# Small matmuls of block inverses alternate between parts of the TensorE array, with another seed of the instruction order

## The chip, the cores and the metric

The kernel runs on one core of a Trainium2 chip. The metric is the device time of one execution in microseconds (us). TensorE is called PE here, VectorE DVE, ScalarE ACT, GpSimd POOL, and SP is the queue that issues the DMAs.

## What is computed

A trunk of two layers over x of 2048 frames by 1024 channels: layer 0 is a gated linear recurrence (RG-LRU), layer 1 a gated DeltaNet with 8 heads of width 128, worked in chunks of 64 frames in the reference. Cut to what matters here, for each head:

```python
a_mat = jnp.where(strict, jnp.einsum('bhncd,bhnmd->bhncm', k_beta, k) * decay_mask, 0.0)
t_mat = lax.linalg.triangular_solve(a_mat + eye, jnp.broadcast_to(eye, a_mat.shape),
                                    left_side=True, lower=True)
w = jnp.einsum('bhncm,bhnmd->bhncd', t_mat, k_beta * jnp.exp(g)[..., None])
u = jnp.einsum('bhncm,bhnmd->bhncd', t_mat, v_beta)
...
def step(state, inp):
    v_new = u_c - jnp.einsum('bhcd,bhde->bhce', w_c, state)
    o_c = jnp.einsum('bhcd,bhde->bhce', q_c, state) + jnp.einsum('bhcm,bhme->bhce', attn_c, v_new)
    state = state * e_c[..., None, None] + jnp.einsum('bhcd,bhce->bhde', k_c, v_new)
```

The change is in how the kernel inverts the unit triangular matrices (`t_mat`), for which it uses blocks of 128 frames.

## The kernel before

Frames are taken in two halves (`u` = 0, 1) of 1024, each half in two tiles (`i`) of 512, each tile in four blocks (`b`) of 128. The big products (`products`, L703: input projections of both layers, tiles `mm`, and output projections, tiles `mmo`) split each operand in a high and a low part and issue three 128x512 matmuls per slice of 128. They fill most of PE's queue, and everything else is put between them: the gates of layer 0 (`pg`, L835), the products of keys and queries (`pkk`, `pqk`, L1172, L1260), the recurrence over blocks (`pp`, `py`, `pS`, L1415 to L1445), and the block inverses.

The inverses of one head and one half (`u`, `h`; there are 16 such pairs) run in two threads. `inverses_thread` solves the 32x32 diagonal blocks on DVE (L1295, L1298). `levels_thread` then joins blocks: 32 to 64, and 64 to 128, for all 8 blocks of 128 (2 tiles x 4 blocks) together. It has four rounds on PE, each written to one PSUM bank (tag `c`, two buffers) and emptied by ACT and DVE before the next:

- `px` (L1337): 16 matmuls of 32x32, 8 with operands in rows 0 to 31 (`a` = 0, output in partitions 32 to 63) and 8 in rows 64 to 95 (`a` = 64, output in partitions 96 to 127). Ahead of it DVE transposes the diagonal blocks in six steps (L1330); the last two of them make the operand of `a` = 64. ACT (L1340) empties the first part, DVE (L1342) the second.
- `pr` (L1349, L1352): 24 matmuls of 32x32. `a` = 0 reads rows 32 to 63 and writes partitions 0 to 31, and L1352 reads the same rows and writes partitions 32 to 63; `a` = 64 reads rows 96 to 127 and writes partitions 64 to 95. `a` = 0 and L1352 need ACT's copy, `a` = 64 needs DVE's.
- `px2` (L1366, named `px` in the profile): 8 matmuls of 64x64, all rows 0 to 63 to partitions 64 to 127. ACT (L1368) empties tile 0, DVE (L1370) tile 1.
- `pr2` (L1376, named `pr` in the profile): 8 matmuls of 64x64, all rows 64 to 127 to partitions 0 to 63. The 4 of tile 0 need ACT's copy, the 4 of tile 1 need DVE's. DVE (L1379) and ACT (L1382) empty it.

Each fp32 matmul of the code stands as two matmul records and two weight loads in the profile, so a round of 16 shows 32.

The order of instructions on each engine is fixed when the program is built. Each piece of work is a generator, and `yield "pe", 1.02` says that the next piece needs PE for 1.02 us by the planner's table. `Weave.run` always takes the thread that can start first by its own clock, and appends its instructions to their engines' queues. `SEED` starts a random sequence that scatters the planner's durations of all engines but PE by 1% (`SPREAD`), so another seed gives another order of the whole program. On the chip each engine works through its queue in that order and waits where a semaphore says so.

Of the kernel before, what the change touches and what calls it, by code (L numbers as in the profile page):

```python
# [13 lines left out]
ALU = mybir.AluOpType  # L14
# [8 lines left out]
NTC = T // TC  # L23
TB = TC // P
# [13 lines left out]

LAG = {"pe": 0.2, "act": 0.128, "dve": 0.113, "pool": 0.034}
WEIGHTS = 0.12  # L40
SEED, SPREAD = 58, 0.01
TABLE = 1.28
TRANSFER = {"sp": (1.56, 0.61, 0.05), "st": (0.74, 0.38, 0.5)}
SHARED = {"dve2": "pool2", "pool2": "dve2"}
# [126 lines left out]
def trunk_kernel(ctx, tc, x, head, small, ada_w, ada_b, final_g, w1, gate_w, ow1, w2, wab, ow2, out):  # L171
    nc = tc.nc
    act, dve, pool, pe, sp = nc.scalar, nc.vector, nc.gpsimd, nc.tensor, nc.sync
# [87 lines left out]
    def tile_(shape, tag, name, dtype=F32):  # L261
        p, n = tags[tag]
        return pools[p].tile(shape, dtype, tag=tag, name=name, bufs=n)
# [4 lines left out]
    def ev(*key):  # L268
        return events.setdefault(key, Event())

    def put(tag, token):
        w.put(slots[tag], token)
# [553 lines left out]
    def gates_thread(u, n, i):  # L826
        xf, ftok = yield ev("xf", u, n, i)
        gw = yield ev("gw", u, n)
        if (u, n, i) == (NU - 1, KT - 1, NTC - 1):
            w.set(ev("lasthalves"))  # L830
        for g in range(2):
            ctok = yield slots["c"]
            yield "pe", 0.86
            pg = ps.tile([P, TC], F32, tag="c", name="pg")
            pe.matmul(pg, lhsT=gw[:, g, :], rhs=xf, start=True, stop=True)  # L835
            w.spawn(gate_thread(u, n, i, g, pg, ctok), 3)
        w.set(ev("gated", u, n, i))
        tr, rtok = yield ev("gate1", u, n, i, 0)
        ti, itok = yield ev("gate1", u, n, i, 1)
        htok = yield slots["th"]  # L840
        yield "act", 0.723, LAG["act"], "exp"
        th = tile_([P, TC], "th", "th")
        act.activation(th, tr, AF.Tanh, bias=sp2[:, n:n + 1], scale=sp2[:, n:n + 1])
        yield "act", 0.724, LAG["act"], "exp"
        act.activation(tr, tr, AF.Exp, bias=sp4n[:, n:n + 1], scale=sp4n[:, n:n + 1])
        yield "dve2", 0.599
        dve.scalar_tensor_tensor(th, tr, 1.0, th, ALU.add, ALU.mult)
        yield "dve2", 0.599
        dve.scalar_tensor_tensor(tr, th, 2.0, th, ALU.subtract, ALU.mult)
        yield "pool2", 0.696  # L850
        pool.tensor_scalar(th, th, -1.0, 1.0, ALU.mult, ALU.add)
        yield "dve2", 0.599
        dve.scalar_tensor_tensor(ti, ti, 1.0, xf, ALU.add, ALU.mult)
        put("xf1", ftok)
        yield "act", 0.54, LAG["act"], "sqrt"
        act.activation(tr, tr, AF.Sqrt, scale=-0.25)
        if u + i > 0:
            yield ev("hcar", n, u * NTC + i - 1)
        yield "dve2", 0.603
        dve.tensor_tensor(ti, ti, tr, ALU.mult)  # L860
        put("tg", rtok)
        yield "dve2", 1.19
        init = 0.0 if u + i == 0 else hcar[:, n:n + 1]
        dve.tensor_tensor_scan(out=ti, data0=th, data1=ti, initial=init, op0=ALU.mult, op1=ALU.add)
        put("th", htok)
        yield "pool", 0.546
        pool.tensor_copy(out=hcar[:, n:n + 1], in_=ti[:, TC - 1:TC])
        w.set(ev("hcar", n, u * NTC + i))
        tz, ztok = yield ev("tz", u, n, i)
        yield "dve2", 0.601  # L870
        dve.tensor_tensor(tz, tz, ti, ALU.mult)
        put("tg", itok)
        yield "st", 1.1
        t0 = u * T + i * TC
        sp.dma_start(out=y_d[n * P:(n + 1) * P, t0:t0 + TC], in_=tz)
        put("tz", ztok)
        w.set(ev("y", u, n, i))

    def gate_thread(u, n, i, g, pg, ctok):
        tok = yield slots["tg"]  # L880
        yield "act", 0.593, LAG["act"], "exp"
        tg = tile_([P, TC], "tg", "tg")
        act.activation(tg, pg, AF.Tanh, bias=gb_s[:, g, n:n + 1], scale=0.5)
        put("c", ctok)
        w.set(ev("gate1", u, n, i, g), (tg, tok))
# [424 lines left out]
    def levels_thread(u, h):  # L1310

        tt_d = yield ev("tt", u, h)
        acs = []
        for i in range(NTC):
            acs.append((yield ev("key", u, h, i))[2])
            for b in range(4):
                yield "sp", 0.016, i == NTC - 1 and b == 3
                q0 = b * NB + i * TB
                sp.dma_start(out=acs[i][32 * b:32 * b + 32, :, 32 * b:32 * b + 32],
                             in_=tt_d[q0:q0 + TB].rearrange("c j i -> j c i"))  # L1320
        chunks = [(i, b, acs[i][:, b, :]) for i in range(NTC) for b in range(TB)]
        ftok = yield slots["tf"]
        yield "pool", 0.391
        tf = tile_([P, NTC, TB, 64], "tf", "tf")
        pool.memset(tf[0:32, :, :, 32:64], 0.0)
        for b in range(3):
            for i in range(NTC):
                yield "dve", 0.199
                o = 32 * (b % 2)
                dve.transpose(out=tf[32 * b:32 * b + 32, i, :, o:o + 32],  # L1330
                              in_=acs[i][32 * b:32 * b + 32, :, 32 * b:32 * b + 32])
        ctok = yield slots["c"]
        yield "pe", 1.02
        px = ps.tile([P, NTC, TB, 32], F32, tag="c", name="px")
        for a in (0, 64):
            for i, b, ac in chunks:
                pe.matmul(px[a + 32:a + 64, i, b, :], lhsT=ac[a:a + 32, a + 32:a + 64],  # L1337
                          rhs=tf[a:a + 32, i, b, 0:32], start=True, stop=True)
        yield "act", 0.282
        act.activation(tf[32:64, :, :, 0:32], px[32:64], AF.Copy, scale=-1.0)  # L1340
        yield "dve", 0.349
        dve.tensor_scalar(tf[96:128, :, :, 0:32], px[96:128], -1.0, None, ALU.mult)  # L1342
        put("c", ctok)
        ctok = yield slots["c"]
        yield "pe", 1.2
        pr = ps.tile([P, 2, NTC, TB, 32], F32, tag="c", name="pr")
        for a in (0, 64):
            for i, b, ac in chunks:
                pe.matmul(pr[a:a + 32, 0, i, b, :], lhsT=tf[a + 32:a + 64, i, b, 0:32],  # L1349
                          rhs=ac[a + 32:a + 64, a + 32:a + 64], start=True, stop=True)  # L1350
                if a == 0:
                    pe.matmul(pr[32:64, 1, i, b, :], lhsT=ac[32:64, 32:64], rhs=tf[32:64, i, b, 0:32],  # L1352
                              start=True, stop=True)
        yield "act", 0.27
        act.copy(tf[32:64, :, :, 0:32], pr[32:64, 1])
        yield "act", 0.163
        act.copy(acs[0][64:96, :, 96:128], pr[64:96, 0, 0])
        for i, a in ((0, 0), (1, 0), (1, 64)):
            yield "dve", 0.197
            dve.tensor_copy(out=acs[i][a:a + 32, :, a + 32:a + 64], in_=pr[a:a + 32, 0, i])  # L1360
        put("c", ctok)
        ctok = yield slots["c"]
        yield "pe", 0.928
        px = ps.tile([P, NTC, TB, 64], F32, tag="c", name="px2")
        for i, b, ac in chunks:
            pe.matmul(px[64:128, i, b, :], lhsT=ac[0:64, 64:128], rhs=tf[0:64, i, b, :], start=True, stop=True)  # L1366
        yield "act", 0.286
        act.activation(tf[64:128, 0], px[64:128, 0], AF.Copy, scale=-1.0)  # L1368
        yield "dve", 0.347
        dve.tensor_scalar(tf[64:128, 1], px[64:128, 1], -1.0, None, ALU.mult)  # L1370
        put("c", ctok)
        ctok = yield slots["c"]
        yield "pe", 0.928
        pr = ps.tile([P, NTC, TB, 64], F32, tag="c", name="pr2")
        for i, b, ac in chunks:
            pe.matmul(pr[0:64, i, b, :], lhsT=tf[64:128, i, b, :], rhs=ac[64:128, 64:128], start=True, stop=True)  # L1376
        put("tf", ftok)
        yield "dve", 0.335
        dve.tensor_copy(out=acs[0][0:64, :, 64:128], in_=pr[0:64, 0])  # L1379
        w.set(ev("inv", u, h, 0))  # L1380
        yield "act", 0.271
        act.copy(acs[1][0:64, :, 64:128], pr[0:64, 1])  # L1382
        w.set(ev("inv", u, h, 1))
        put("c", ctok)

# [403 lines left out]
```

## Time and profile before

| what | value |
|---|---|
| median of 3 runs | 1878.76 us (1876.84 to 1879.47) |
| the profiled execution's own time | 1877.61 us |
| its span, first to last instruction | 1875.9 us |
| PE busy | 1831.7 us, 98% |
| weight loads busy | 1472.3 us, 78% |
| DVE, ACT, POOL busy | 1347.0, 1163.4, 359.6 us |
| mean granted TensorE clock | 0.995 |

A row of the timeline gives start (us), length (us), engine, line, operation, output<-inputs, shape, and a count; in brackets the engine's idle time before it and what ended it. Records of PE overlap: the next one starts before the modelled end of the last, so the distance between starts, not the length of a record, says what PE's queue paid. Rows of the same line that follow one another are merged.

### The profile page before, as it was taken

To read this page: it belongs to the slowest core of one execution; us is meant where nothing else is said; L and a number is where in the kernel's file an instruction comes from. 1 tells how busy PE (TensorE), PEld (TensorE's weight loads), DVE (VectorE), ACT (ScalarE), POOL (GpSimd) and SP (SyncE) were. 2 spreads that over 40 slices of the span, in tenths; PEclk is the share of its full clock that TensorE was granted. 3 is DMA by queue.
4 is the path that set the end of the run, shared out by engine and by line. 5 is a ranking of instruction groups with operands and counts; after the bars stand their busy time and mean duration, and the time that the engine had idled before them with its cause. 6 is when DMAs were issued, how large, how long until landed. Compare 5 with 4: busy or idle time off the path is not lost.

```text
span 1875.9 us, 30928 instructions
## 1 busy us (share of the span) xinstructions
PE 1831.7 (98%) x10222; PEld 1472.3 (78%) x10222; DVE 1347.0 (72%) x3121; ACT 1163.4 (62%) x2703; POOL 359.6 (19%) x896
## 2 busy tenths in 40 slices
PE   6999999999999999999999999999999999999998
PEld 4777777777888877887887877788888888887887
DVE  7889897776455648777788877667676677776653
ACT  4655777666211467787777766786778787754221
POOL 1111110011000013132422221131222222311010
PEclk9999999999999999999999999999999999999999
DMA  8467756554588545467677656356654655686841
GB/s 352 140 196 209 231 178 211 171 166 133 194 221 222 186 125 147 130 179 186 154 168 178 146 147 206 106 136 153 156 137 123 158 142 147 153 235 193 252 145 68
DMA packets 510425, 322.75 MB, mean 172 GB/s; under 512 B 369844, under 2 KB 437940, under 8 KB 510264
## 3 DMA queue, kind: packets, MB, share of 16 engines
q1 hardware_dynamic: 510264, 320.77, 60.6%
q8 instruction: 81, 1.33, 0.3%
q14 instruction: 80, 0.66, 0.1%
HBM read 219.93 MB, written 100.73 MB: 171 GB/s over the span
## 4 chain that ended last, share of the span: by engine, by line
PE 75%; DVE 7%; DMA 6%; ACT 6%; issue 2%; SPq 2%; POOL 2%; DVEq 0%; POOLq 0%; ACTq 0%
PE mm L703 40%; PE mmo L703 18%; DMA raw<-in_w 3%; PE pg L835 3%; DMA oraw<-in_ow 2%; PE py L1432 1%; PE pp L1415 1%; PE pS L1445 1%; PE pS L1444 1%; PE pqk L1260 1%; PE pp L1416 1%; PE adaps L372 1%; PE pkk L1172 1%; PE pab L1058 1%; DVE xf L755 1%
## 5 line engine op out<-in xcount | busy, mean ns | idle before, releaser
L755 DVE SCALAR_TENSOR_TENSOR xf<-xe,small_s,xf 128x512 f32<-128x512 f32 x288 | 214.3, 750 | 32.0 <-ACT xf L1013 28.8
L679 ACT CAST whi<-raw 128x1024 fp32r<-128x1024 f32 x96 | 100.2, 1043 | 55.5 <-DMA raw<-in_w 52.1
L1295 DVE TENSOR_TENSOR ttmp<-blk,tblk 128x60 f32<-128x60 f32 (+24 forms) x496 | 106.0, 214 | 19.4 <-DMA o_d<-ob 4.5
L1298 DVE TENSOR_TENSOR tblk<-tblk,ttmp 128x60 f32<-128x60 f32 (+24 forms) x496 | 106.3, 214 | 12.4
L703 PE MATMUL mm<-hh_('in2', 0)_4993,whi 128*128 128x512 f32 x256 | 105.2, 411 | 0.0
L703 PE MATMUL mm<-hh_('in2', 1)_11807,wlo 128*128 128x512 f32 x256 | 104.8, 409 | 0.0
L703 PE MATMUL mm<-hl_('in2', 1)_11604,whi 128*128 128x512 f32 x256 | 104.7, 409 | 0.0
L703 PE MATMUL mm<-hh_('in2', 1)_11603,wlo 128*128 128x512 f32 x256 | 104.7, 409 | 0.0
L703 PE MATMUL mm<-hh_('in2', 0)_4993,wlo 128*128 128x512 f32 x256 | 104.4, 408 | 0.0
L703 PE MATMUL mm<-hh_('in2', 1)_11603,whi 128*128 128x512 f32 x256 | 104.2, 407 | 0.0
L703 PE MATMUL mm<-hl_('in2', 0)_4994,whi 128*128 128x512 f32 x256 | 103.8, 406 | 0.0
L703 PE MATMUL mm<-hl_('in2', 1)_11808,whi 128*128 128x512 f32 x256 | 103.8, 405 | 0.0
L703 PE MATMUL mm<-hh_('in2', 1)_11807,whi 128*128 128x512 f32 x256 | 103.8, 405 | 0.0
L703 PE MATMUL mm<-hh_('in2', 0)_5108,wlo 128*128 128x512 f32 x256 | 103.5, 404 | 0.0
L703 PE MATMUL mm<-hl_('in2', 0)_5109,whi 128*128 128x512 f32 x256 | 103.0, 403 | 0.0
L703 PE MATMUL mm<-hh_('in2', 0)_5108,whi 128*128 128x512 f32 x256 | 103.0, 402 | 0.0
L703 PE MATMUL mmo<-ol,oh 128*128 128x512 f32 (+1 forms) x264 | 102.7, 389 | 0.0
L703 PE MATMUL mmo<-oh,ol 128*128 128x512 f32 (+1 forms) x264 | 102.7, 389 | 0.0
L703 PE MATMUL mmo<-oh,oh 128*128 128x512 f32 (+1 forms) x264 | 102.6, 389 | 0.0
L703 PE MATMUL mmo<-oh,yl 128*128 128x512 f32 x256 | 100.8, 394 | 0.0
L703 PE MATMUL mmo<-oh,yh 128*128 128x512 f32 x256 | 100.8, 394 | 0.0
L703 PE MATMUL mmo<-ol,yh 128*128 128x512 f32 x256 | 100.4, 392 | 0.0
(314 smaller groups left out, 5388.0 us busy)
## 6 DMA issues: line engine op xcount, KB each, us to landing
raw<-in_w SPq DMA_DIRECT2D x96, 512.0 KB, 4.2
araw<-in_ada_w SPq DMA_DIRECT2D x32, 512.0 KB, 4.4
xt<-x_d SPq DMA_DIRECT2D x32, 512.0 KB, 4.8
xt_d<-xb SPq DMA_DIRECT2D x192, 64.0 KB, 2.7
xk<-xt_d SPq DMA_DIRECT2D x24, 512.0 KB, 6.5
xt<-in_x SPq DMA_DIRECT2D x16, 512.0 KB, 5.6
ada<-in_ada_w SPq DMA_DIRECT2D x16, 512.0 KB, 10.2
y_d<-tz SPq DMA_DIRECT2D x32, 256.0 KB, 4.8
```

The costliest lines, as they stand in the source:

```text
L372: pe.matmul(pt, lhsT=c_bc[:, k, :], rhs=raw[:, k, :], start=(k == 0), stop=(k == KT - 1))
L679: act.copy(hi, raw)
L703: pe.matmul(pt, lhsT=lhs[a][:, k, :], rhs=rhs[b][:, k, :], start=(k == 0 and n == 0), stop=(k == KT - 1 and n == 2))
L755: dve.scalar_tensor_tensor(xf, xe[:, 1 + j:1 + j + TC], wc[:, j:j + 1], xf, ALU.mult, ALU.add)
L835: pe.matmul(pg, lhsT=gw[:, g, :], rhs=xf, start=True, stop=True)
L1058: pe.matmul(pab, lhsT=whl[:, k, :], rhs=hpr[q][:, k, :], start=(k == 0 and q == 0), stop=(k == KT - 1 and q == 1))
L1172: pe.matmul(pkk[:, b, :], lhsT=kc, rhs=kc, start=True, stop=True)
L1260: pe.matmul(pqk[:, b, :], lhsT=kt[:, b * P:(b + 1) * P], rhs=qt[:, b * P:(b + 1) * P], start=True, stop=True)
L1295: dve.tensor_tensor(tmp, blk[:, j, j + 1:32].unsqueeze(2).to_broadcast([P, r, c_]), t[:, j, 0:c_].unsqueeze(1).to_broadcast([P, r, c_]), A ...
L1298: dve.tensor_tensor(t[:, j + 1:32, 0:c_], t[:, j + 1:32, 0:c_], tmp, ALU.subtract)
L1415: pe.matmul(pp[:, 0, :], lhsT=kc, rhs=S_, start=True, stop=True)
L1416: pe.matmul(pp[:, 1, :], lhsT=qc, rhs=S_, start=True, stop=True)
```

## The change

The order of the matmuls in the four rounds is changed. `chunks` runs over blocks outside and tiles inside; in `px` and `pr` the two row parts (`a` = 0 and `a` = 64) follow each other for each block, where before all of `a` = 0 came first. In `px2` and `pr2` the outputs of tile 0 and tile 1 go to different partition halves of the bank, so consecutive matmuls alternate between them; DVE's L1370 then reads partitions 0 to 63 and writes 64 to 127, and ACT's L1382 reads 64 to 127 and writes 0 to 63. The planner's durations of the four rounds and of the gates are edited, and the seed is another. Number and shape of the matmuls are as before.

```diff
-SEED, SPREAD = 58, 0.01
+SEED, SPREAD = 120, 0.01
...
-            yield "pe", 0.86
+            yield "pe", 0.856
             pg = ps.tile([P, TC], F32, tag="c", name="pg")
...
-        chunks = [(i, b, acs[i][:, b, :]) for i in range(NTC) for b in range(TB)]
+        chunks = [(i, b, acs[i][:, b, :]) for b in range(TB) for i in range(NTC)]
...
-        yield "pe", 1.02
+        yield "pe", 0.7
         px = ps.tile([P, NTC, TB, 32], F32, tag="c", name="px")
-        for a in (0, 64):
-            for i, b, ac in chunks:
+        for i, b, ac in chunks:
+            for a in (0, 64):
                 pe.matmul(px[a + 32:a + 64, i, b, :], lhsT=ac[a:a + 32, a + 32:a + 64],
                           rhs=tf[a:a + 32, i, b, 0:32], start=True, stop=True)
...
-        yield "pe", 1.2
+        yield "pe", 0.92
         pr = ps.tile([P, 2, NTC, TB, 32], F32, tag="c", name="pr")
-        for a in (0, 64):
-            for i, b, ac in chunks:
+        for i, b, ac in chunks:
+            for a in (0, 64):
                 pe.matmul(pr[a:a + 32, 0, i, b, :], lhsT=tf[a + 32:a + 64, i, b, 0:32],
                           rhs=ac[a + 32:a + 64, a + 32:a + 64], start=True, stop=True)
-                if a == 0:
-                    pe.matmul(pr[32:64, 1, i, b, :], lhsT=ac[32:64, 32:64], rhs=tf[32:64, i, b, 0:32],
-                              start=True, stop=True)
+            pe.matmul(pr[32:64, 1, i, b, :], lhsT=ac[32:64, 32:64], rhs=tf[32:64, i, b, 0:32], start=True, stop=True)
...
-        yield "pe", 0.928
+        yield "pe", 0.66
         px = ps.tile([P, NTC, TB, 64], F32, tag="c", name="px2")
         for i, b, ac in chunks:
-            pe.matmul(px[64:128, i, b, :], lhsT=ac[0:64, 64:128], rhs=tf[0:64, i, b, :], start=True, stop=True)
+            pe.matmul(px[64 - 64 * i:128 - 64 * i, i, b, :], lhsT=ac[0:64, 64:128], rhs=tf[0:64, i, b, :], start=True, stop=True)
...
-        dve.tensor_scalar(tf[64:128, 1], px[64:128, 1], -1.0, None, ALU.mult)
+        dve.tensor_scalar(tf[64:128, 1], px[0:64, 1], -1.0, None, ALU.mult)
...
-        yield "pe", 0.928
+        yield "pe", 0.66
         pr = ps.tile([P, NTC, TB, 64], F32, tag="c", name="pr2")
         for i, b, ac in chunks:
-            pe.matmul(pr[0:64, i, b, :], lhsT=tf[64:128, i, b, :], rhs=ac[64:128, 64:128], start=True, stop=True)
+            pe.matmul(pr[64 * i:64 * i + 64, i, b, :], lhsT=tf[64:128, i, b, :], rhs=ac[64:128, 64:128], start=True, stop=True)
...
-        act.copy(acs[1][0:64, :, 64:128], pr[0:64, 1])
+        act.copy(acs[1][0:64, :, 64:128], pr[64:128, 1])
```

The next pieces are the programs' own order, one engine each, before any run; `[waits DVE_49]` is a wait for DVE's counter, and lines from L1352 on lie 1 to 2 lower in the changed file. PE's queue at the first `px` round, before:

```order
L703 MATMUL mm<-hl_('in2', 0)_4994,whi 128x512
L1337 MATMUL px<-tf,ac 32x32 [waits DVE_49]
L1337 MATMUL px<-tf,ac 32x32 x3
L1337 MATMUL px<-tf,ac 32x32 [waits DVE_49]
L1337 MATMUL px<-tf,ac 32x32 x3
L1337 MATMUL px<-tf,ac 32x32 [waits DVE_49]
L1337 MATMUL px<-tf,ac 32x32 x3
L1337 MATMUL px<-tf,ac 32x32 [waits DVE_49]
L1337 MATMUL px<-tf,ac 32x32 x3
L703 MATMUL mm<-hh_('in2', 0)_4993,wlo 128x512
```

The same place, now:

```order
L703 MATMUL mm<-hl_('in2', 0)_4994,whi 128x512
L1337 MATMUL px<-tf,ac 32x32 [waits DVE_49] x2
L1337 MATMUL px<-tf,ac 32x32
L1337 MATMUL px<-tf,ac 32x32 [waits DVE_49]
L1337 MATMUL px<-tf,ac 32x32 x12
L703 MATMUL mm<-hh_('in2', 0)_4993,wlo 128x512
```

The waits for the last two transposes, which stood ahead of the 9th and the 13th matmul, stand ahead of the 2nd and the 4th. PE's queue at the first `pr` round, before (the second wait for DVE is that for the operand of `a` = 64; rows between are left out):

```order
L1349 MATMUL pr<-ac,tf 32x32 [waits DMAHW6_49,Activation_49]
L1352 MATMUL pr<-tf,ac 32x32
L1349 MATMUL pr<-ac,tf 32x32
...
L1349 MATMUL pr<-ac,tf 32x32 [waits DMAHW2_49]
...
L1349 MATMUL pr<-ac,tf 32x32 [waits DMAHW0_49,DVE_49]
L1349 MATMUL pr<-ac,tf 32x32 x3
L1349 MATMUL pr<-ac,tf 32x32 [waits DMAHW4_49]
```

The same place, now:

```order
L1349 MATMUL pr<-ac,tf 32x32 [waits DMAHW6_49,Activation_49]
L1349 MATMUL pr<-ac,tf 32x32 [waits DMAHW0_49,DVE_49]
L1351 MATMUL pr<-tf,ac 32x32
L1349 MATMUL pr<-ac,tf 32x32 [waits DMAHW2_49]
L1349 MATMUL pr<-ac,tf 32x32 [waits DMAHW4_49]
L1351 MATMUL pr<-tf,ac 32x32
```

The wait for DVE moved from the 17th matmul to the 2nd. What the seed does is seen at the second `px` round on PE, where the neighbours are the recurrence of the head before. Before:

```order
L1445 MATMUL pS<-yt,at 128x128
L703 MATMUL mm<-hh_('in2', 0)_5108,whi 128x512
L703 MATMUL mm<-hl_('in2', 0)_5109,whi 128x512
L1337 MATMUL px<-tf,ac 32x32 [waits Activation_49]
L1337 MATMUL px<-tf,ac 32x32 x7
L1337 MATMUL px<-tf,ac 32x32 [waits DVE_49]
...
L1415 MATMUL pp<-state_97,kt 128x128 [waits DVE_49]
L1416 MATMUL pp<-state_97,qt 128x128
```

Now:

```order
L1413 MATMUL pp<-state_97,kt 128x128 [waits DVE_49]
L1414 MATMUL pp<-state_97,qt 128x128
...
L1430 MATMUL py<-zt,ac 128x128 [waits DMAHW1_49,DVE_49]
L1337 MATMUL px<-tf,ac 32x32 x3
L1337 MATMUL px<-tf,ac 32x32 [waits DVE_49]
L1337 MATMUL px<-tf,ac 32x32 x12
L703 MATMUL mm<-hl_('in2', 0)_4994,whi 128x512
```

The round stood ahead of a recurrence step (`pp`) and stands in the middle of one now, between `py` and `pS`; all engines' queues differ in this way from the first tile of layer 0 on.

## Prediction

> **What bounds the kernel.** I read the page's totals first, then a table by stage, then PE's waits, then the timeline of PE around single rounds.
>
> ```profile
> span 1875.9 us, 30928 instructions
> PE 1831.7 (98%) x10222; PEld 1472.3 (78%) x10222; DVE 1347.0 (72%) x3121; ACT 1163.4 (62%) x2703; POOL 359.6 (19%) x896
> ```
>
> ```profile
> core 0: us, PE busy (x) PEld busy (x) DVE busy (x) ACT busy (x) POOL busy (x), PEclk, DMA share, GB/s
> 39.00:470.00 431.00, 425.71 (x1762) 324.68 (x1761) 357.49 (x598) 284.55 (x392) 59.01 (x82) 1.00 0.59 182
> 470.00:641.00 171.00, 171.00 (x745) 139.56 (x745) 92.08 (x133) 40.82 (x51) 9.39 (x21) 1.00 0.75 219
> 641.00:1721.00 1080.00, 1063.10 (x6974) 873.02 (x6972) 788.81 (x2227) 787.11 (x2160) 267.68 (x722) 1.00 0.60 155
> 1721.00:1869.00 148.00, 147.88 (x667) 121.76 (x666) 80.37 (x93) 34.12 (x74) 15.29 (x43) 1.00 0.52 163
> ```
>
> The second table's columns are the stage, its length, each engine's busy time, PE's granted clock and the DMA share. The four stages are the input projections of layer 0, its output projection, layer 1, and the last output projection. PE stands idle 5.3 us in the first (431 less 425.71), 0, 16.9 and 0.1 us in the others, 22.3 us together. The inverses all lie in layer 1, where DVE and ACT are busy 73% of 1080 us. So PE's queue sets the time, and a microsecond less of PE work there is a microsecond of the span, as long as the other engines follow.
>
> ```profile
> PE px L1337 <- DVE tf L1330: 1.2, 2, 0.6
> PE pr L1349 <- DVE tf L1342: 1.1, 2, 0.8
> ```
>
> PE's waits in the rounds (total us, times, longest) are small now. They become important below.
>
> **What the new order of the matmuls saves.** First a `px` round that waits for nothing.
>
> ```profile
> 1675.39 0.39 PE L703 MATMUL mmo<-oh,oh 128*128 128x512 f32 x1
> 1675.71 1.09 PE L1337 MATMUL px<-tf,ac 32*32 32x32 f32 x32
> 1676.73 0.50 PE L703 MATMUL mmo<-ol,oh 128*128 128x512 f32 x1
> ```
>
> It holds PE's queue for 1676.73 - 1675.71 = 1.02 us. Then a `pr` round, start to end with rows left out:
>
> ```profile
> 1283.77 0.21 PE L1349 MATMUL pr<-ac,tf 32*32 32x32 f32 x1
> 1283.77 0.21 PE L1352 MATMUL pr<-tf,ac 32*32 32x32 f32 x1
> ...
> 1284.17 0.19 PE L1349 MATMUL pr<-ac,tf 32*32 32x32 f32 x1
> 1284.17 0.19 PE L1352 MATMUL pr<-tf,ac 32*32 32x32 f32 x1
> 1284.18 0.21 PE L1349 MATMUL pr<-ac,tf 32*32 32x32 f32 x2
> 1284.21 0.19 PE L1352 MATMUL pr<-tf,ac 32*32 32x32 f32 x1
> 1284.23 0.19 PE L1349 MATMUL pr<-ac,tf 32*32 32x32 f32 x2
> ...
> 1284.27 0.19 PE L1352 MATMUL pr<-tf,ac 32*32 32x32 f32 x1
> 1284.30 0.57 PE L1349 MATMUL pr<-ac,tf 32*32 32x32 f32 x13
> 1284.80 0.50 PE L703 MATMUL mm<-hh_('in2', 1)_11603,wlo 128*128 128x512 f32 x1
> ```
>
> This round already does in part what the change wants everywhere. L1349 with `a` = 0 and L1352 write different column parts of the array and alternate in the code: their 32 records start within 0.50 us, two every 0.032 us. The 16 records of L1349's `a` = 64, in other rows and other columns, come behind them, and three of those start before the other two parts have ended (the rows marked x2, since 13 are left for the last row). There three records start every 0.032 us and none is slowed. Afterwards the 13 that are left take 0.50 us alone. So one part of the array starts a 32x32 record every 0.032 us, parts do not hold each other up, and a part that stands behind a long run of another part starts late.
>
> `px`: two parts of 16 records, now in turn. Like the 32 above, they start within 0.50 us, and 1.02 less the 0.90 between its first and last start (1.09 less 0.19 for a record) leaves 0.12 to the next work. New 0.62, saved 0.40.
>
> `pr`: three parts of 16. All at once 0.51 + 0.12 = 0.63 against 1284.80 - 1283.77 = 1.03: saved 0.40. If only two parts ran at a time it would be 48 records at 0.016, 0.75 + 0.12, saved 0.16. I take 0.40, since the trace shows three at once.
>
> ```profile
> 1287.51 1.14 PE L1366 MATMUL px<-tf,ac 64*64 64x64 f32 x16
> 1288.59 0.50 PE L703 MATMUL mm<-hl_('in2', 1)_11604,whi 128*128 128x512 f32 x1
> ```
>
> `px2` and `pr2`: 1.08 us for 16 records, of which 1.14 less about 0.22 for one record, 0.92, lies between first and last start: 0.061 each. No row shows 64x64 records in two parts. The bounds are nothing saved, and half of the 0.92, 0.46. Nearest are the two column parts of `pr`, which share their rows just as the two halves here do and ran without loss; I take 0.46.
>
> [...]
>
> If nothing were late: 16 x (0.40 + 0.40 + 0.46 + 0.46) = 27.5 us.
>
> **What it takes away.** In the old order the first half of a round ran while the second half's operand was still made. Now the second matmul waits for it.
>
> ```profile
> 757.33 1.38 PE L1337 MATMUL px<-tf,ac 32*32 32x32 f32 x32
> 757.92 0.30 DVE L1330 STREAM_TRANSPOSE tf<-ac 32x128 f32<-32x128 f32 x1
> 758.64 0.50 PE L703 MATMUL mm<-hh_('in2', 0)_4993,wlo 128*128 128x512 f32 x1
> ...
> 1618.09 0.50 DVE L1330 STREAM_TRANSPOSE tf<-ac 32x128 f32<-32x128 f32 x2
> 1618.21 1.09 PE L1337 MATMUL px<-tf,ac 32*32 32x32 f32 x32
> 1619.24 0.50 PE L703 MATMUL mm<-hl_('in2', 1)_11604,whi 128*128 128x512 f32 x1
> ```
>
> In 8 of the 16 `px` rounds the last transpose ended after the round's first matmul had started (the first and the last of the 8 stand here): 758.22 against 757.33, late by 0.89, and 1618.59 against 1618.21, late by 0.38. The 8 latenesses sum to 6.6 us, and these rounds held PE 10.5 us in all (1.31 in the first, 1.03 in the last). With the same lateness the new round lasts the lateness plus about 0.61 (0.05 from the transpose's end to the fourth matmul, 28 records at 0.016, and the 0.12): 6.6 + 8 x 0.61 = 11.5. So late `px` rounds lose 1.0 together, and the other 8 gain 3.2: net 2.2 us instead of 6.4.
>
> ```profile
> 760.23 0.21 PE L1349 MATMUL pr<-ac,tf 32*32 32x32 f32 x1
> 760.38 0.43 DVE L1342 TENSOR_SCALAR tf<-px 32x256 f32<-32x256 f32 x1
> ...
> 1678.82 0.21 PE L1349 MATMUL pr<-ac,tf 32*32 32x32 f32 x1 [0.21 <-ACT tf L1340]
> 1679.72 0.69 PE L1349 MATMUL pr<-ac,tf 32*32 32x32 f32 x16 [0.20 <-DVE tf L1342]
> ```
>
> The same in `pr`, where `a` = 64 needs DVE's L1342: late in 4 of 16 (the first and the last stand here, 0.58 and about 0.84). Those 4 keep nearly their time (saved 0.35 together), 12 save 0.40: 5.2 us.
>
> ```profile
> 766.59 0.43 DVE L1370 TENSOR_SCALAR tf<-px 64x256 f32<-64x256 f32 x1
> 766.63 1.14 PE L1376 MATMUL pr<-ac,tf 64*64 64x64 f32 x16
> ...
> 1685.49 1.32 PE L1376 MATMUL pr<-ac,tf 64*64 64x64 f32 x16
> 1685.65 0.43 DVE L1370 TENSOR_SCALAR tf<-px 64x256 f32<-64x256 f32 x1
> ```
>
> And in `pr2`, where tile 1 needs L1370: late in 4 (first and last here, 0.39 and 0.59); 0.2 + 12 x 0.46 = 5.7 us. `px2` needs ACT's L1355 in every matmul, before and now: 16 x 0.46 = 7.4 us.
>
> Behind a wait stands PE's whole queue, which is in order, so the lateness is paid in full.
>
> **The rest.** Two evacuations (L1370, L1382) now cross partition halves. No row shows that; I take their present durations, and if each took twice its time, some 0.4 us on DVE and on ACT per pair, the idle quarter of both engines would cover it unless the round is late. The changed order adds 4 rows of table loads on ACT (121 to 125):
>
> ```profile
> L1131 ACT ACT_TABLE_LOAD x32 | 41.1, 1283 | 0.5
> ```
>
> At 1.283 us that is 5.1 us, hidden by ACT's 293 us of idle time in layer 1; without that cover it is a loss of 5.1. The seed and the planner's new durations move every instruction, DMAs of the SP queue too, but add no work. Their price lies in the 22.3 us of PE idle: a luckier order takes off at most that, an unluckier one may add as much. No row says which; I take 0, and half of it, 10 us, either way for the range.
>
> **Sum.** 2.2 + 5.2 + 7.4 + 5.7 = 20.5 us. The profiled execution took 1877.61 us for its span of 1875.9; it becomes 1857.1. The median of the three runs, 1878.76, lies 1.15 higher, so the forecast is 1858.
>
> **Rivals.**
> Nothing late (chance 0.15): the new order places the rounds where DVE is done. 27.5 us, 1851. For it: half of `px` and three quarters of `pr` are so now. Against it: an order that makes PE faster leaves DVE less time.
>
> [...]
>
> Slower (0.04): PE, faster than its neighbours, arrives at the second matmul of `px`, `pr` and `pr2` before DVE each time. There are 48 such places; from 0.43 us more lateness on average at each, the 20.5 us are gone, and at 0.6 us it is 1887. For it: `px` is late in half its rounds already. Against it: three quarters of `pr` and `pr2` are not.
>
> The new order eats most: an added idle time near 22 us gives no change (0.05), about 13 us gives 1871 (0.09).
>
> **Numbers.** The forecast itself, 1848 to 1868 with the order's 10 us, has 0.55. Faster by over 0.2% (3.8 us, about what can be told from no change here) are the forecast, nothing late, no overlap and the eaten gain: 0.55 + 0.15 + 0.12 + 0.09 = 0.91. Same 0.05, slower 0.04. The range reaches to 1871, to hold the partial cases, and down to 1847.
>
> **What would show it.** Right: undisturbed `px` rows x32 of about 0.70 us with the next work 0.62 behind their start, `pr` at 0.63, 64x64 rows x16 of about 0.68 with 0.61 to the next; records of different parts alternating; PE idle of layer 1 not far from 17 us, with more in the waits for L1330 and L1342. Wrong: 64x64 records still 0.06 us apart, or waits for DVE in the rounds of 20 us in sum, or idle elsewhere that grew with the order.

## The result: 1854 us, 1.3% faster, and the profile after

The changed kernel takes 1854.09 us (median of 4 runs, 1852.01 to 1858.81) against 1878.69 for the kernel before (4 runs): ratio 0.9874, 95% interval 0.9853 to 0.9895. The profiled execution took 1852.01 us, with a mean granted clock of 0.997. In the changed file the lines from L1351 on lie 1 to 2 lower than before: `px2` is L1364, `pr2` L1374, its operand for tile 1 comes from L1368, the recurrence is L1413 to L1443.

The page's totals after:

```profile
span 1849.5 us, 30915 instructions
PE 1805.3 (98%) x10222; PEld 1445.4 (78%) x10222; DVE 1342.6 (73%) x3121; ACT 1169.4 (63%) x2707; POOL 351.0 (19%) x896
```

PE's busy time fell by 26.4 us, the span by 26.4. The four stages of the changed kernel, in the columns of the prediction's table:

```profile
39.00:470.00 431.00, 427.78 (x1770) 325.76 (x1770) 356.89 (x600) 295.96 (x401) 50.21 (x82) 1.00 0.59 184
470.00:641.00 171.00, 171.00 (x745) 139.55 (x744) 92.24 (x132) 38.17 (x48) 8.15 (x21) 1.00 0.75 216
641.00:1697.00 1056.00, 1037.18 (x6982) 846.84 (x6982) 784.88 (x2227) 784.82 (x2158) 269.26 (x722) 1.00 0.61 159
1697.00:1843.00 146.00, 145.53 (x657) 119.80 (x655) 80.66 (x93) 33.71 (x72) 15.13 (x43) 1.00 0.49 157
```

Layer 1 lasts 1056 us where it lasted 1080; the stages ahead of it end at the same times as before. Its PE idle time is 18.8 us (1056 less 1037.18), against 16.9.

Rounds that wait for nothing, in the timeline of PE of the changed kernel:

```profile
1654.07 0.69 PE L1337 MATMUL px<-tf,ac 32*32 32x32 f32 x32
1654.69 0.50 PE L703 MATMUL mmo<-oh,oh 128*128 128x512 f32 x1
...
1662.79 0.68 PE L1364 MATMUL px<-tf,ac 64*64 64x64 f32 x16
1663.41 0.50 PE L703 MATMUL mmo<-oh,oh 128*128 128x512 f32 x1
```

`px` holds the queue for 0.62 us (1654.69 less 1654.07), where it held it for 1.02; `px2` for 0.62 where it held it for 1.08 (`pr2`, not shown, is like it: 0.61 in 11 of 16 rounds). And `pr`, with rows left out:

```profile
1107.69 0.22 PE L1349 MATMUL pr<-ac,tf 32*32 32x32 f32 x2
1107.70 0.21 PE L1351 MATMUL pr<-tf,ac 32*32 32x32 f32 x1
...
1108.20 0.19 PE L1351 MATMUL pr<-tf,ac 32*32 32x32 f32 x1
1108.32 0.50 PE L703 MATMUL mm<-hh_('in2', 0)_4993,wlo 128*128 128x512 f32 x1
```

Three records, one of each part, start every 0.032 us, from the first row to the last before L703, so the round lasts 0.63 us (1108.32 less 1107.69) instead of 1.03.

What the change took away shows too. The longest wait in a round, PE first and then DVE:

```profile
1276.21 0.32 PE L1374 MATMUL pr<-ac,tf 64*64 64x64 f32 x2
1278.07 0.68 PE L1374 MATMUL pr<-ac,tf 64*64 64x64 f32 x14 [1.54 <-DVE tf L1368]
1278.67 0.50 PE L703 MATMUL mm<-hh_('in2', 1)_11798,wlo 128*128 128x512 f32 x1
```

```profile
1276.47 0.75 DVE L755 SCALAR_TENSOR_TENSOR xf<-xe,small_s,xf 128x512 f32<-128x512 f32 x1
1277.14 0.18 DVE L1295 TENSOR_TENSOR ttmp<-blk,tblk 128x28 f32<-128x28 f32 x1
1277.36 0.21 DVE L1298 TENSOR_TENSOR tblk<-tblk,ttmp 128x28 f32<-128x28 f32 x1
1277.60 0.42 DVE L1368 TENSOR_SCALAR tf<-px 64x256 f32<-64x256 f32 x1
```

The two records of tile 0's first matmul start at 1276.21. The second matmul is tile 1's, and its operand comes from L1368, which stands on DVE behind three instructions of other threads and ends at 1278.02. The round takes 2.46 us. In the old order three more matmuls of tile 0 would have run in that time.

The sums over all 16 rounds of a kind, from a round's first record to the next other matmul (differences rounded last):

| kind | before, us | after, us | saved | forecast |
|---|---|---|---|---|
| `px` | 18.7 | 14.0 | 4.6 | 2.2 |
| `pr` | 17.3 | 12.3 | 5.1 | 5.2 |
| `px2` | 17.1 | 9.8 | 7.3 | 7.4 |
| `pr2` | 17.9 | 12.9 | 5.0 | 5.7 |
| sum | 71.0 | 49.0 | 22.0 | 20.5 |

### The profile page after: what moved, and what is told of

It is laid out like the page before. It is cut to its first block, busy times and chain, and to the rows that moved or that the text cites. A ratio compares the mean times of both kernels' runs of the same rounds, so it can differ in the third digit from the quotient of the medians.

```text
span 1849.5 us, 30915 instructions
## 1 busy us (share of the span) xinstructions
PE 1805.3 (98%) x10222; PEld 1445.4 (78%) x10222; DVE 1342.6 (73%) x3121; ACT 1169.4 (63%) x2707; POOL 351.0 (19%) x896
## 3 DMA queue, kind: packets, MB, share of 16 engines
q8 instruction: 80, 1.31, 0.3%
## 4 chain that ended last, share of the span: by engine, by line
PE 65%; DMA 10%; DVE 9%; ACT 8%; SPq 4%; issue 3%; POOL 1%; DVEq 0%; POOLq 0%; ACTq 0%
PE mm L703 34%; PE mmo L703 18%; DMA raw<-in_w 3%; PE pg L835 2%; DVE xf L755 2%; PE py L1430 1%; PE pS L1443 1%; PE pS L1442 1%; PE pp L1413 1%; PE pp L1414 1%; DMA oraw<-in_ow 1%; PE adaps L372 1%; ACT whi L679 1%; SPq L1319 1%; PE pqk L1260 1%
## 5 line engine op out<-in xcount | busy, mean ns | idle before, releaser
L679 ACT CAST whi<-raw 128x1024 fp32r<-128x1024 f32 x96 | 100.0, 1042 | 59.4 <-DMA raw<-in_w 58.8
L703 PE MATMUL mm<-hh_('in2', 1)_11798,whi 128*128 128x512 f32 x256 | 105.1, 410 | 0.0
L703 PE MATMUL mm<-hh_('in2', 1)_11579,wlo 128*128 128x512 f32 x256 | 104.4, 408 | 0.0
L703 PE MATMUL mm<-hh_('in2', 0)_4993,wlo 128*128 128x512 f32 x256 | 104.3, 407 | 0.0
L703 PE MATMUL mm<-hh_('in2', 1)_11579,whi 128*128 128x512 f32 x256 | 104.1, 407 | 0.0
L703 PE MATMUL mm<-hh_('in2', 1)_11798,wlo 128*128 128x512 f32 x256 | 104.0, 406 | 0.0
L703 PE MATMUL mm<-hl_('in2', 0)_4994,whi 128*128 128x512 f32 x256 | 104.0, 406 | 0.0
L703 PE MATMUL mm<-hh_('in2', 0)_5108,whi 128*128 128x512 f32 x256 | 103.6, 405 | 0.0
L703 PE MATMUL mm<-hl_('in2', 1)_11580,whi 128*128 128x512 f32 x256 | 103.3, 404 | 0.0
L703 PE MATMUL mm<-hh_('in2', 0)_4993,whi 128*128 128x512 f32 x256 | 103.2, 403 | 0.0
L703 PE MATMUL mm<-hh_('in2', 0)_5108,wlo 128*128 128x512 f32 x256 | 103.1, 403 | 0.0
L703 PE MATMUL mmo<-oh,oh 128*128 128x512 f32 (+1 forms) x264 | 103.0, 390 | 0.0
L703 PE MATMUL mmo<-oh,ol 128*128 128x512 f32 (+1 forms) x264 | 102.8, 389 | 0.0
L703 PE MATMUL mm<-hl_('in2', 0)_5109,whi 128*128 128x512 f32 x256 | 102.6, 401 | 0.0
L703 PE MATMUL mm<-hl_('in2', 1)_11799,whi 128*128 128x512 f32 x256 | 102.6, 401 | 0.0
L703 PE MATMUL mmo<-ol,oh 128*128 128x512 f32 (+1 forms) x264 | 102.1, 387 | 0.0
L703 PE MATMUL mmo<-oh,yh 128*128 128x512 f32 x256 | 100.8, 394 | 0.0
L703 PE MATMUL mmo<-oh,yl 128*128 128x512 f32 x256 | 100.8, 394 | 0.0
L703 PE MATMUL mmo<-ol,yh 128*128 128x512 f32 x256 | 100.3, 392 | 0.0
```

What stands on the lines that cost most here:

```text
L679: act.copy(hi, raw)
L703: pe.matmul(pt, lhsT=lhs[a][:, k, :], rhs=rhs[b][:, k, :], start=(k == 0 and n == 0), stop=(k == KT - 1 and n == 2))
```

## The experiments

The change has two parts that can be told apart: the rounds' inner order, and the order of the whole program (seed and planned durations). None of the kernels below leaves out any of the computation. Ratios are to runs of the kernel before on the same chip. To read them I split the stretch from 39 us to PE's last matmul of each profiled execution into three: PE's idle time, what PE lost while its granted clock was 0.50 (an estimate: half of the time in these stretches), and the rest, which is PE's busy time at full clock. The three add up to the length. Half of the idle time inside the stretches at 0.50 is in the clock's loss too, so the loss is too large there and the busy time at full clock too small: by 3 us with seed 200, by 7 with short plans, by 0 to 2.6 in the others.

| kernel | ratio (95% interval) | length | busy at full clock | idle | lost to the clock |
|---|---|---|---|---|---|
| before | 1 | 1829.9 | 1802.6 | 22.2 | 5.1 |
| after | 0.9874 (0.9853 to 0.9895) | 1803.5 | 1779.8 | 22.0 | 1.7 |
| alternation alone | 0.9970 (0.9956 to 0.9984) | 1820.3 | 1781.3 | 30.5 | 8.5 |
| order alone | 0.9926 (0.9908 to 0.9944) | 1817.5 | 1799.0 | 13.3 | 5.1 |
| 32-wide rounds alone | 0.9988 (0.9972 to 1.0005) | 1822.3 | 1792.9 | 22.5 | 6.8 |
| 64-wide rounds alone | 0.9969 (0.9954 to 0.9983) | 1828.3 | 1792.2 | 27.5 | 8.5 |
| old seed, new durations | 0.9971 (0.9955 to 0.9986) | 1824.9 | 1777.2 | 35.8 | 11.9 |
| new seed, old durations | 0.9963 (0.9947 to 0.9979) | 1820.3 | 1780.9 | 32.6 | 6.8 |
| seed 7 | 0.9929 (0.9902 to 0.9957) | 1817.7 | 1773.5 | 30.6 | 13.7 |
| order of seed 7, old rounds | 1.0017 (1.0004 to 1.0030) | 1830.6 | 1798.1 | 22.3 | 10.2 |
| seed 200 | 1.0047 (1.0028 to 1.0066) | 1840.2 | 1777.3 | 40.7 | 22.2 |
| order of seed 200, old rounds | 1.0142 (1.0117 to 1.0166) | 1851.9 | 1800.2 | 32.9 | 18.8 |
| short plans, seed 200 | 1.0077 (1.0061 to 1.0093) | 1845.1 | 1768.8 | 42.1 | 34.1 |

The last four columns come from one execution each, the ratios from all. The clock's loss differs between executions of one kernel by several us (the mean granted clock of 28 runs of the kernel before goes from 0.990 to 0.998), so a difference of 3.4 us in that column shows nothing by itself.

**The alternation alone.** The kernel before with the five edits of the matmuls and the two of the evacuations; seed, planned durations and so the order on every engine are those of before.

```diff
-        chunks = [(i, b, acs[i][:, b, :]) for i in range(NTC) for b in range(TB)]
+        chunks = [(i, b, acs[i][:, b, :]) for b in range(TB) for i in range(NTC)]
...
-        for a in (0, 64):
-            for i, b, ac in chunks:
+        for i, b, ac in chunks:
+            for a in (0, 64):
...
-            pe.matmul(px[64:128, i, b, :], lhsT=ac[0:64, 64:128], rhs=tf[0:64, i, b, :], start=True, stop=True)
+            pe.matmul(px[64 - 64 * i:128 - 64 * i, i, b, :], lhsT=ac[0:64, 64:128], rhs=tf[0:64, i, b, :], start=True, stop=True)
```

> The alternation of all four rounds alone: seed, planner's durations and with them every engine's order of instructions are those of before. Theory A (parts of the array run at once, PE's queue is the bound): rounds that wait for nothing take 0.62 (px), 0.63 (pr), 0.61 (px2, pr2) us, and with the latenesses of before's order the sum of my forecast holds, 20.5 us: 1858 us, range 1854 to 1865. In the late px rounds the new order is no faster than the old: the first one, at about 757 us, takes 1.4 to 1.6 us where it took 1.31. Rival B (the other seed and the planner's durations made the gain, the alternation little): 1874 to 1879 us.

Measured: 1872.05 us, ratio 0.9970. The rounds got shorter by 16.4 us (`px` 1.7, `pr` 5.0, `px2` 7.0, `pr2` 2.6), but only about 5.6 us of it arrived in the time, which lies between the ranges of both theories. PE's waits there (total us, times, longest):

```profile
PE px L1337 <- DVE tf L1330: 3.9, 7, 0.9
PE pr L1374 <- DVE tf L1368: 3.4, 5, 1.1
...
PE px L1364 <- DVE ac L1358: 2.8, 2, 2.6
...
PE py L1430 <- DVE zt L1422: 2.3, 5, 1.1
...
PE pr L1374 <- ACT tf L1366: 1.6, 1, 1.6
```

In the kernel before, in the same order, these five are 1.2, 0.2, 2.3, 0.2 and 0.3 us. The first `px` round of this kernel shows the price that the prediction worked out:

```profile
759.83 0.61 PE L1337 MATMUL px<-tf,ac 32*32 32x32 f32 x6
760.79 0.62 PE L1337 MATMUL px<-tf,ac 32*32 32x32 f32 x26 [0.35 <-DVE tf L1330]
761.35 0.50 PE L703 MATMUL mm<-hh_('in2', 0)_4993,wlo 128*128 128x512 f32 x1
```

It lasts 1.52 us (761.35 less 759.83); before it lasted 1.31. In the profiled execution PE idles 8.3 us more, and loses 3.4 us more to the clock. The second part is not borne out by all runs: their mean granted clock is 0.9939, and 0.9940 in the runs of the kernel before beside them.

**The order alone.** The changed kernel, with seed 120 and the new planned durations, but the matmuls inside the rounds as before.

```diff
-        for i, b, ac in chunks:
-            for a in (0, 64):
+        for a in (0, 64):
+            for i, b, ac in chunks:
...
-            pe.matmul(pr[64 * i:64 * i + 64, i, b, :], lhsT=tf[64:128, i, b, :], rhs=ac[64:128, 64:128], start=True, stop=True)
+            pe.matmul(pr[0:64, i, b, :], lhsT=tf[64:128, i, b, :], rhs=ac[64:128, 64:128], start=True, stop=True)
```

> The order of instructions of the changed kernel on every engine (seed 120, new planner durations), with the matmuls inside the four rounds as before (one part after the other). Theory A: rounds take 1.02, 1.03, 1.08, 1.08 us again; of the 24.6 us between the medians the rounds explain 22.0 (sums of the time they held PE, before less after), so the order alone is worth about 2.6 us: 1876, range 1871 to 1881. Rival B: 1854 to 1860 us.

Measured: 1865.12 us, ratio 0.9926, outside both ranges, with rounds that last 68.8 us in all, nearly as before (71.0). Idle time is 13.3 us. So more than half of the change's gain is there without any change in the rounds, and the alternation added to this order brings the ratio from 0.9926 to 0.9874.

**One width at a time.** In the order of before, only `px` and `pr` alternate in the one kernel, only `px2` and `pr2` in the other (the edits are those of the alternation alone, taken apart).

> Only px and pr alternate (32x32), px2 and pr2 as before; order of instructions of before. Theory A: px gains 2.2 to 4.6, pr 5.1 us: 1869 to 1872. Rival C (a round's gain is eaten by waits elsewhere, so that the parts of the change do not add up): under 4 us, 1875 to 1879.

> Only px2 and pr2 alternate (64x64, partition halves), px and pr as before; order of instructions of before. Theory A: px2 gains 7.4, pr2 5.0 to 5.7 us: 1865 to 1867, and with the experiment on the 32-wide rounds alone the gains add to that of all four. Rival C: under 6 us, 1873 to 1879.

Measured: 0.9988 for the 32-wide rounds, which can't be told from no change, and 0.9969 for the 64-wide ones. In the profiled executions PE's busy time at full clock fell by 9.7 and 10.4 us, together about the 21.3 of the alternation alone. Neither part is without effect on PE, and neither brings much of it to the end, as rival C had it.

**Seed or durations.** The changed kernel with the seed of before (58), and with the planned durations of before.

```diff
-SEED, SPREAD = 120, 0.01
+SEED, SPREAD = 58, 0.01
```

```diff
-            yield "pe", 0.856
+            yield "pe", 0.86
...
-        yield "pe", 0.7
+        yield "pe", 1.02
...
-        yield "pe", 0.92
+        yield "pe", 1.2
...
-        yield "pe", 0.66
+        yield "pe", 0.928
...
-        yield "pe", 0.66
+        yield "pe", 0.928
```

> The changed kernel (alternation, new planner durations) with the seed of before, 58. Theory D, formed on the first four runs: the alternation shortens the rounds as forecast, but where the planner still believes in the old durations PE runs ahead of its plan and the saved time comes back as waits for DVE and ACT; the planner has to be told. Then most of the gain is here with any seed: 1853 to 1863 us, PE idle in layer 1 about 15 us. Rival E (seed 120 is a lucky draw worth about 12 us): 1864 to 1872, idle about 25 us as in the alternation alone.

> The changed kernel with seed 120, but the planner's durations of before (1.02, 1.2, 0.928, 0.928, gates 0.86). Theory D: as in the alternation alone PE runs ahead of its plan: 1864 to 1874 us, late px and pr2 rounds, PE idle in layer 1 about 25 us. Rival E: 1852 to 1860.

Measured: 1873.36 and 1870.67 us, ratios 0.9971 and 0.9963. That is what the alternation gives in the order of before (0.9970). Neither the new durations nor the seed is worth anything alone: PE idles 35.8 and 32.6 us in them, and 22.0 with both. That the planner has truer durations does not make the order better. Theory D misses the first of the two by 10 us, rival E the second.

**Other seeds.** The changed kernel with seeds 7 and 200, the number being the only edit.

> The changed kernel with an arbitrary seed, 7. Theory D: 1853 to 1865 us; a draw costs a few us of PE idle. Rival E: 1864 to 1876.

> The changed kernel with another arbitrary seed, 200. Theory D: 1853 to 1865 us. Rival E: 1864 to 1876.

Measured: 1864.29 us (0.9929) and 1887.90 us (1.0047). With 120 and 58 that makes four programs that differ in one number: 1854, 1864, 1873 and 1888 us, a spread of 34 us, more than the whole change. The slowest of them is slower than the kernel before, and lies outside both ranges given for it. With the old rounds three of these orders were run (below), and they rank alike: seed 120's is the fastest, then seed 7's, and seed 200's the slowest. PE's waits with seed 200:

```profile
PE pqk L1260 <- ACT qt L1020: 6.4, 4, 3.0
PE py L1430 <- DVE zt L1422: 5.4, 8, 1.7
PE px L1337 <- DVE tf L1330: 5.0, 6, 1.7
PE pS L1442 <- ACT yt L1436: 4.1, 9, 1.0
PE pp L1413 <- DVE state L1455: 3.5, 8, 0.5
```

In the changed kernel the same five are 1.9, 1.3, 2.4, 2.2 and 0.7 us. What lies behind three of them is seen in PE's queue with seed 200:

```profile
1154.86 0.49 PE L1413 MATMUL pp<-state,kt 128*128 128x128 f32 x2 [0.44 <-DVE state L1455]
1155.19 0.39 PE L1414 MATMUL pp<-state,qt 128*128 128x128 f32 x2
1156.05 0.49 PE L1430 MATMUL py<-zt,ac 128*128 128x128 f32 x2 [0.48 <-DVE zt L1422]
1156.91 0.49 PE L1442 MATMUL pS<-yt,kd 128*128 128x128 f32 x2 [0.37 <-ACT yt L1436]
...
1160.34 0.79 PE L1442 MATMUL pS<-yt,kd 128*128 128x128 f32 x2 [0.37 <-ACT yt L1436]
```

The steps of the recurrence follow one another with no product of L703 between them, so PE waits 0.4 us for DVE or ACT at each. There are 20 such bare steps in this order, with 8.5 us of idle time; in the kernel before there is none, in the changed one there are 3, without a wait. With the old rounds the order of seed 200 has the same 20, with 8.7 us, so they come with the order and not with the alternation. From 1159 us on the records are longer (0.79 us for L1442 at 1160.34, 0.49 at 1156.91), and the clock is lower: 0.93 on average in the 5 us to 1160, 0.52 in the 10 us from there.

**Shorter plans.** Seed 200, and the planner told that the rounds take 0.3 to 0.35 us, less than they do, in the hope that the other engines get more time between them. With seed 120 the same plan gave no kernel and so no time; the expectation below means that one by "the run before".

```diff
-        yield "pe", 0.7
+        yield "pe", 0.3
...
-        yield "pe", 0.92
+        yield "pe", 0.35
...
-        yield "pe", 0.66
+        yield "pe", 0.31
...
-        yield "pe", 0.66
+        yield "pe", 0.31
```

> As the run before, with seed 200, whose order was the slowest (1888 us, 41 us idle). Theory G: 12 to 22 us idle, 1840 to 1855. Rival E: 1855 to 1890.

Measured: 1893.22 us, ratio 1.0077, idle 42.1 us, and the rounds last 59.4 us in all. The idle time did not fall, and the time is not better than with the plan of the change (1.0047). The clock is also lower, 0.980 on average over its runs. The theory that short plans leave the other engines time is not borne out.

**The orders of seeds 200 and 7 with the old rounds.** As in the order alone, with another seed; they give what the alternation is worth in two more orders.

> The order of instructions of the changed kernel with seed 200 on every engine, with the matmuls inside the rounds as before. Rounds 69 us instead of 51. Theory G: PE is 2 us per head behind its plan, idle falls from 41 us to 13 to 22: 1875 to 1885, that is no slower than with the alternation in spite of 18 us more work. Rival H (alternation shortens the time by its rounds in any order): 1900 to 1908.

> The order of instructions of the changed kernel with seed 7 on every engine, with the matmuls inside the rounds as before: a fourth pair at equal order. Theory I (at equal order the alternation gains its shorter rounds, some 15 to 20 us, less what comes back as PE idle and low clock, 0 to 12 us, by the order): 6 to 18 us slower than seed 7 with alternation, ratio to before 0.996 to 1.003, 1871 to 1884 us. Rival G (a plan that PE lags behind has less idle, enough to make up for it): at or below 0.993, 1864 us or less.

Measured: 1903.81 us (1.0142) and 1880.85 us (1.0017). So theory G, that PE behind its plan idles less, misses both, and theory H and theory I hold. The four pairs with one order each, with old and with alternating rounds. The rows are those of PE's stretch from 39 us to its last matmul; first the order of before, then those of seeds 120, 7 and 200:

```profile
39.00:1869.00 1830.00, 1807.69 (x10142) 1459.03 (x10140) 1318.75 (x3049) 1146.61 (x2674) 351.36 (x868) 1.00 0.60 168
```

```profile
39.00:1859.40 1820.40, 1789.80 (x10142) 1435.08 (x10140) 1317.52 (x3049) 1145.56 (x2674) 350.82 (x868) 1.00 0.61 169
```

```profile
39.00:1856.50 1817.50, 1804.14 (x10143) 1459.82 (x10141) 1313.74 (x3048) 1152.67 (x2678) 342.00 (x868) 1.00 0.61 169
```

```profile
39.00:1842.60 1803.60, 1781.50 (x10148) 1431.95 (x10147) 1314.27 (x3050) 1152.66 (x2678) 342.76 (x868) 1.00 0.61 170
```

```profile
39.00:1869.80 1830.80, 1808.34 (x10144) 1461.53 (x10142) 1318.39 (x3050) 1152.67 (x2678) 350.57 (x868) 0.99 0.60 168
```

```profile
39.00:1856.70 1817.70, 1787.12 (x10142) 1435.39 (x10140) 1316.99 (x3048) 1154.12 (x2678) 352.77 (x868) 0.99 0.60 169
```

```profile
39.00:1890.90 1851.90, 1819.01 (x10142) 1468.54 (x10140) 1317.23 (x3048) 1159.48 (x2684) 351.72 (x868) 0.99 0.59 166
```

```profile
39.00:1879.20 1840.20, 1799.47 (x10143) 1441.78 (x10141) 1316.14 (x3048) 1159.50 (x2684) 350.46 (x868) 0.99 0.60 167
```

The second number is the length and the third PE's busy time. Their difference is the idle time (the windows end up to 0.2 us behind the last matmul, so the numbers here are those of the table above), and it grows by about 8 us in each pair: 22.2 to 30.5, 13.3 to 22.0, 22.3 to 30.6, 32.9 to 40.7. The busy time at full clock falls by 21.3, 19.2, 24.6 and 22.9 us. The lengths fall by 9.6, 13.9, 12.9 and 11.7 us; by the ratios it is 5.6, 9.8, 16.5 and 17.8 us, in the mean 12.4, each of them uncertain by 3 to 6 us. So the alternation gains in each of the four orders, about 12 us, and somewhat less than half of what it saves on PE comes back, some 8 us of it as idle time. The clock's loss changes by +3.4, -3.4, +3.4 and +3.4 us in these single executions. Over all runs the mean granted clock goes from 0.9940 to 0.9939, from 0.9962 to 0.9952, from 0.9913 to 0.9912 and from 0.9863 to 0.9878, so a loss that the alternation brings with it is not shown.

**How far a part of the array runs ahead.** The kernel before, with `px` in runs of two matmuls for each row part, `px2` in runs of two for each output half, and `pr2` still in its four and four, but to two halves; `pr` is as before. It ran once, so there is no interval.

```diff
+        twos = [chunks[q] for q in (0, 1, 4, 5, 2, 3, 6, 7)]
...
-        for a in (0, 64):
-            for i, b, ac in chunks:
+        for i, b, ac, a in [(*c, a) for q in range(0, NTC * TB, 2) for a in (0, 64) for c in chunks[q:q + 2]]:
...
-        for i, b, ac in chunks:
-            pe.matmul(px[64:128, i, b, :], lhsT=ac[0:64, 64:128], rhs=tf[0:64, i, b, :], start=True, stop=True)
+        for i, b, ac in twos:
+            pe.matmul(px[64 - 64 * i:128 - 64 * i, i, b, :], lhsT=ac[0:64, 64:128], rhs=tf[0:64, i, b, :], start=True, stop=True)
```

> Order of instructions of before; px goes in runs of two matmuls (four records) per part, px2 in runs of two per half, pr2 in runs of four (eight records) per half, pr as before. Read from the rounds that wait for nothing. Theory P (a part of the array takes three records ahead behind the one that runs, as the first records of the third part in pr and of the second in px showed before): runs of two cost nothing, px 0.62 to 0.66, px2 0.61 to 0.66, and in pr2 the second half starts when the first has three left, about 0.85 us. Rival (records of two parts overlap only where they follow each other directly): px above 0.75, px2 above 0.75, pr2 about 1.05.

Measured, in PE's timeline of this kernel:

```profile
788.75 0.71 PE L1337 MATMUL px<-tf,ac 32*32 32x32 f32 x32
789.39 0.38 PE L1415 MATMUL pp<-state,kt 128*128 128x128 f32 x1
...
1515.46 0.73 PE L1366 MATMUL px<-tf,ac 64*64 64x64 f32 x16
1516.12 0.50 PE L703 MATMUL mm<-hh_('in2', 1)_11807,wlo 128*128 128x512 f32 x1
...
1518.86 0.96 PE L1376 MATMUL pr<-ac,tf 64*64 64x64 f32 x16
1519.75 0.50 PE L703 MATMUL mm<-hl_('in2', 1)_11808,whi 128*128 128x512 f32 x1
```

Runs of two matmuls (four records) cost `px` 0.64 us against 0.62 in strict turns, and `px2` 0.66 against 0.62. Runs of four (eight records) cost `pr2` 0.89, between 0.61 and the 1.07 of one half alone. Eight records of one half take about 8 x 0.058 us; if the other half can start three records ahead, the round saves 3 x 0.058 = 0.17 us of its 1.07 and lasts 0.90. That agrees with the 0.89. So in these rounds a part starts about three records ahead of its turn, and a run of four records overlaps with the next nearly in full (0.02 and 0.04 us longer than in strict turns). The whole kernel took 1873.83 us in its one run.

## Why the prediction was right, and which of its steps were not

**The rounds: right.** The undisturbed rounds came out at 0.62, 0.63, 0.61 to 0.62 and 0.61 us, where 0.62, 0.63 and, for the 64-wide, 0.61 to 0.62 followed from the rows of before. The value taken for the 64-wide rounds, from the column parts of `pr`, held: two column parts on the same rows ran side by side (0.62 us for `px2`, where one half alone took 1.08).

**The lateness: right in kind, wrong in place.** In the order of before, for which it was worked out, the four terms measured 1.7, 5.0, 7.0 and 2.6 us against 2.2, 5.2, 7.4 and 5.7. `pr2` was mis-sized: 6 of its 16 rounds were late, by 0.26 to 1.46 us beyond the 0.61, where the four counted before were expected to stay as they were. In the new order they measured 4.6, 5.1, 7.3 and 5.0, since this order puts the rounds where fewer are late: 5 of 16 in `px`, where 8 were counted before and 9 are in the alternation alone, and 5 in `pr2`, four of them by no more than 0.72 us. At an equal order the sum would have been 16.4, four less than forecast.

**A microsecond of PE is a microsecond of the span: wrong.** The prediction held this "as long as the other engines follow", and counted lateness inside the rounds alone. At an equal order 10 to 14 us of the 19 to 25 saved arrive in the profiled executions (9.6, 13.9, 12.9, 11.7), 12.4 on average by the ratios. PE's idle time grows by 8 us each time, in the order of before at the rounds' own waits and at others such as `py` for DVE. DVE and ACT, 73% busy in layer 1, did not follow a faster PE everywhere.

**The order at 0, and 10 us either way: wrong.** It was worth 13.9 us by its ratio alone (1878.7 x 0.0074), and 12.4 us in the profiled execution, outside the bounds that I had set, though inside the 22 us named as the most that it could take off. The same 22 us were named as the most that an unluckier order might add, and that bound failed too: with the old rounds the order of seed 200 adds 26.7 us (1878.7 x 0.0142). Over the four seeds of the changed kernel the spread is 34 us. No row that I read told this; the bounds were too narrow for a draw of this width.

So that the forecast came out 4 us from the measured time was luck: two errors were of opposite sign. In this order the alternation brings 9.8 us by the ratios where 20.5 were forecast, and the order takes off 13.9 where 0 was. PE's idle time stands at 22 us before and after for that reason, and not because nothing happened to it.

**Rivals.** No run shows the "no overlap" that has 0.12 among the prediction's chances; the rows show the contrary: `px2` at 1662.79 reads the same rows in all its records, and takes 0.62 us instead of 1.08, and the three parts of `pr`, which go to one PSUM tile, take 0.63 instead of 1.03. Nothing late did not come about, 22.0 us instead of 27.5 in the rounds. A late second matmul each time did not come about either, but 1.54 us at 1276.21 shows its price. That the new order eats most of the gain did not happen with seed 120; seed 200 (1.0047) shows that an order can. The ACT table loads, 125 where there were 121 as forecast, do not show as a loss: PE's waits for ACT sum to 10.7 us where they were 11.6. The evacuations across halves take as long as before (DVE 0.418 us on average against 0.428, ACT 0.368 against 0.366).

**Open.** That seed 200's order has bare recurrence steps explains 8.5 of the 18.7 us of idle time by which it exceeds the changed kernel; which places make up the rest, and what in the planner's choice leads to them, was not settled. No run says how seed 120 compares with more than three others, so its 13.9 us may be the worth of a picked draw. Four orders are too few for a mean of the alternation's worth beyond "about 12 us". Whether the rounds' new waits could be taken away by moving L1330 and L1368 forward on DVE was not tried.

## What to carry to other kernels

Small matmuls that use different row or column parts of the array should take turns matmul by matmul, or in runs of two; strict turns shortened these rounds by two fifths (1.02, 1.03 and 1.08 us to 0.62, 0.63 and 0.62), and runs of two came to 0.64 and 0.66. When PE gets faster at a fixed order of instructions, expect part of the saving to come back as waits for its neighbours (8 us of idle time in each of the four orders here): measure idle time beside busy time, and look at the wait moved ahead by the alternation itself. A change that also draws a new static order has to be split from it, and run in several orders, before a gain of one per cent is put down to the change.

## What the hardware showed that I had not expected

The clock. In these kernels PE's granted clock falls to 0.50 in stretches of 3.4 us and longer ones, such as 6.8 us from 25.9 us on in the kernel before and 10.2 us from 783.8 us on with seed 200. In the changed kernel there is one between 39 us and PE's last matmul, behind the wait of L1090:

```profile
675.12 0.41 PE L1090 MATMUL pgc<-gg,upper 128*128 128x64 f32 x2 [2.66 <-DVE gg L1085]
...
677.73 0.63 PE L703 MATMUL mm<-hh_('in2', 0)_4993,wlo 128*128 128x512 f32 x1
```

The windows around it, with PE's clock in the third column from the end:

```profile
673.00:676.30 3.30, 1.18 (x8) 0.99 (x9) 3.06 (x10) 0.96 (x3) 0.18 (x1) 1.00 0.00 0
676.30:679.70 3.40, 3.40 (x9) 2.57 (x10) 3.40 (x6) 2.09 (x5) 0.10 (x1) 0.50 0.45 168
679.70:683.00 3.30, 3.30 (x16) 2.69 (x15) 2.24 (x3) 1.86 (x3) 0.00 (x0) 1.00 0.20 61
```

A product's record lasts 0.63 us there instead of 0.39, though PE does not idle any more; L703's matmuls start 0.43 us apart from 677.73 on, where ahead of the wait they start 0.23 us apart. The clock fell 1.2 us after the end of 2.66 us of idle time (676.3 against 675.12). With seed 200 the clock is low for 44.4 us in all, and PE is busy in 38.5 of them; half of that, 19 us, is my estimate of what it costs. There the stretch from 1159 us follows the bare steps, whose single waits are 0.4 us, not one long one. Both falls come behind idle time; that the idle time brings them, and so costs more than itself, was not shown. The clock also falls where PE has not idled, as the kernel before shows:

```profile
1161.30:1169.30 8.00, 8.00 (x113) 5.74 (x112) 4.81 (x13) 3.69 (x11) 1.55 (x4) 1.00 0.59 175
1169.30:1172.70 3.40, 3.40 (x10) 2.62 (x9) 2.51 (x5) 3.28 (x8) 0.00 (x0) 0.51 0.00 0
```

PE is busy for all 8.00 us ahead of this fall. Two of the rounds and other small matmuls lie there; whether they are the reason was not tried.

Two other things came out of the rows above. In `pr` three parts of the array each start a 32x32 record every 0.032 us, writing one PSUM tile, and none slows the others: the 13 records that one part ran alone, at 1284.30 in the kernel before, start 0.032 us apart too. And in these rounds a part starts about three records ahead of its turn, so the order in which the matmuls are issued decided how far parts overlapped: `pr2` took 1.07 us in one half alone, 0.89 in runs of four matmuls to each half, and 0.61 in turns.
